# Seven products by token halves, differences in place, a bias table stored head by head, and a final norm in another order

## The chip, the cores and the metric

The kernel runs on one core of one Trainium2 chip. Its time is in device microseconds (us); runs of one kernel mostly agree within 0.3%. A core has a matrix engine (TensorE; PE in the rows, its weight loads PEld), a vector engine (VectorE, DVE), an activation engine (ScalarE, ACT), GpSimd (POOL) and SyncE (SP), which here issues every DMA. The engines run side by side, each works through its own list in order, and one that needs another's result waits at a semaphore. One DMA is shared out over up to 16 DMA engines.

## The reference, cut to what matters

One decoder layer on 1024 tokens of width 1024: a mixer sub-layer (pooling, and sparse attention with a relative bias), attention to a memory, and a SwiGLU feed-forward layer, each between two RMSNorms and added to the residual. The change touches three places:

```python
def _rmsnorm(x, g):
    y = xf * lax.rsqrt(jnp.mean(xf * xf, axis=-1, keepdims=True) + EPS)
    return (y * g).astype(x.dtype)
...
        bias = rel_bias_table[_t5_bucket(q_pos[None, :, None] - sel)]   # 8 heads, 32 buckets
        logits = logits + jnp.moveaxis(bias, -1, 1)
...
def _swiglu(h, w_gate_up, w_down):          # D_MODEL 1024, D_FF 2816
    g, u = jnp.split(h @ w_gate_up, 2, axis=-1)
    return (jax.nn.silu(g) * u) @ w_down
...
        h = _rmsnorm(x, norm_ffn_pre)
        x = x + _rmsnorm(_swiglu(h, w_gate_up, w_down), norm_ffn_post)
```

All of it is float32. The kernel splits each operand into a high and a low part and makes every product from three matmuls (high x high, high x low, low x high).

## The kernel before, in words

**Order.** Nothing is issued as it is written. A recorder (`Recorder`) notes each operation with its tiles, and a planner (`schedule`) then makes one list per engine: of the operations whose inputs are ready by its own costs it takes, for each engine, the earliest in program order that has its buffers. It prices a DMA by its bytes alone (`total * 4 / 360.0` ns). Large tiles share 42 slots of 4 KB per partition (`slot`), weights on their way have two buffers for the high part (`whi`) and two for the low (`wlo`), and 512-column products have four PSUM banks (`bank`). Since every operation is issued by one helper line, all rows carry L139; tiles are told by their names (a row leaves out trailing digits).

**The start.** Blocks of 128 tokens are normed and transposed (`pt_n`). Then come the indexer's key and queries (`o_ki`, `o_qi`); their halves are copied across partitions by DMAs (`kih`, `kil`, `qi`), after which the indexer's scores (`sc`) are made. Everything later on TensorE stands behind the first `sc` in its list. Beside this GpSimd builds one row of 383 biases for each of the 8 heads (`brow`, on 8 partitions), and a DMA writes each row 128 times to DRAM (`rowd`, 1024 rows of 1532 bytes). Attention reads it back some 300 us later (`Bn`). The weights of the pooling branch (`r_wu`) come on the same queue.

**Gate and up.** The layer's first product is done with seven half-size products instead of eight (the Winograd form of Strassen's method). The weight tile of 128 columns `f` (22 of them) gives seven weight operands; the activations are cut into B11, B21 (one half of the tokens, first and second 512 channels) and B12, B22 (the other half), and into the differences T1 = B12 - B11, T2 = B22 - T1, T3 = B22 - B12, T4 = B21 - T2. Each of the seven is split (`spread`: ScalarE high, VectorE low). In the kernel before, a token half holds every other block of 128 tokens (`divmod(b, 2)`), so blocks 0 to 3 give the first 256 columns of all seven and blocks 4 to 7 the second 256. So that TensorE has work before the last blocks are closed, the first two weight tiles (`CUT = 2`) are multiplied 256 columns at a time; the other 20 take 512 columns. One weight tile is seven products of 12 matmuls into three banks (`ga`, `gb`, `gc`). Seven weight operands of each of the first four tiles were prepared earlier and stored; `fetch` loads all seven of a tile in one go (`uw`, 512 KB each).

**Closing a block.** `close` takes the memory output `z` of a block, norms it (`j_pb`, `me_pb`, `rs_pb`), adds the residual (`zb`), stores it (`x2d`), norms it again (`j_nb`, `xn_nb`), transposes it (`pt_nb`), and ScalarE copies the transposes to `h3B..x`.

**The end.** `w_down` is multiplied in six pieces; in the last each block gets its sum (`acc`, in halves of 512), squares on ScalarE (`jf`), the gain (`acc * g6`, 1024 wide, in place, hence after both squares), the mean and power on GpSimd (`mef`, `rf`), and two multiply-adds with the residual (`x2r`) that are stored.

Of the kernel before, what the change touches and what calls it, by code (L numbers as in the profile page):

```python
# [17 lines left out]
P = 128  # L18
# [322 lines left out]
def hybrid_block_kernel(ctx: ExitStack, tc: tile.TileContext, x, mem, norm_mix_pre, norm_mix_post,  # L341
# [140 lines left out]
    class WinoT:  # L482

        TYPES = ("B11", "T2", "T1", "T3", "B21", "T4", "B22")

        def __init__(self, name):
            self.name, self.hl, self.src = name, {}, {}

        def k(self, t, c, s):
            return self.hl[t][0][c // 2][:, c % 2, s], self.hl[t][1][c // 2][:, c % 2, s]

        def close(self, src, g, b, name):
            r = rstd_of(src, name)
            xn = slot([P, D], F32, f"xn_{name}")
            apply_norm(xn, src, r, g)
            t, h = divmod(b, 2)
            v, u = divmod(t, 2)
            if h == 0 and u == 0:  # L500
                self.src[v] = {B: slot([P, 4, 2, P], F32, f"{self.name}{B}x{v}") for B in ("B11", "B21", "B12", "B22")}
            for q in range(2):
                pt = bank([P, 4, P], f"pt_{name}{q}")
                for c in range(4):
                    nc.tensor.transpose(pt[:, c], xn[:, (4 * q + c) * P:(4 * q + c + 1) * P], ident)
                nc.scalar.activation(self.src[v][f"B{q + 1}{h + 1}"][:, :, u], pt, AF.Copy)
            if h == 1 and u == 1:
                B = self.src[v]
                for T, a, b_ in (("T1", "B12", "B11"), ("T2", "B22", "T1"), ("T3", "B22", "B12"), ("T4", "B21", "T2")):
                    B[T] = slot([P, 4, 2, P], F32, f"{self.name}{T}x{v}")  # L510
                    nc.vector.tensor_tensor(B[T], B[a], B[b_], op=OP.subtract)

        def spread(self, v):
            s = slice(v * 256, (v + 1) * 256)
            for t in self.TYPES:
                if v == 0:
                    self.hl[t] = [[slot([P, 2, 512], F32R, f"{self.name}{t}{w}{j}") for j in range(2)] for w in "hl"]
                for j in range(2):
                    split(self.hl[t][0][j][:, :, s], self.hl[t][1][j][:, :, s],
                          self.src[v][t][:, 2 * j:2 * j + 2].rearrange("p c u t -> p c (u t)"))  # L520

# [102 lines left out]
    while u < span:  # L624
# [251 lines left out]

    def fetch(f):
        shapes = [[P, KC, P]] * 2 + [[P, 2, 4, P]] * 5
        ts = []
        nc.ahead = nc.SHORT  # L880
        for j, shape in enumerate(shapes):
            if j < 2:
                t = nc.tile(sb, shape, F32R, name=f"uw{f}{j}", tag=("whi", "wlo")[j], bufs=2)
            else:
                t = slot(shape, F32R, f"uw{f}{j}")
            v = f32(t) if j < 2 else f32(t).rearrange("p a c m -> p (a c) m")
            nc.sync.dma_start(v, unitd[f, j])
# [3 lines left out]

    def operands(ts):
        gh, gl, h12, l12, h34, l34, a22 = ts
        return dict(A11=(gh[:, :4], gl[:, :4]), A12=(gh[:, 4:], gl[:, 4:]), A22=(a22[:, 0], a22[:, 1]),
                    S1=(h12[:, 0], l12[:, 0]), S2=(h12[:, 1], l12[:, 1]),
                    S3=(h34[:, 0], l34[:, 0]), S4=(h34[:, 1], l34[:, 1]))
# [114 lines left out]

    units = [(i, g) for i in range(NB) for g in range(2)]
    ready = {units[0]: attn_soft(*units[0])}
    for k, (u, nxt) in enumerate(zip(units, units[1:] + [None])):
        if nxt:
            ready[nxt] = attn_soft(*nxt)
        attn_pv(*u, ready.pop(u))
        if k < 8 and k + GFIRST < KC:
            attn_gate(k + GFIRST)
        if k >= 8:  # L1020
            proj_attn(0, [k - 8])
    proj_attn(1, range(KC))
# [43 lines left out]


    KVm = [slot([P, D], F32R, f"{n}n{w}_") for n in "KV" for w in "hl"]
    for j in range(4):
# [89 lines left out]

    aTd = nc.tile(dr, [NF, P, 2, 512], F32, name="aTd", tag="aTd", dram=True)  # L1160

    def mmk(o, wh, wl, act, t, s, first):
        for c in range(4):
            ah, al = act.k(t, c, s)
# [4 lines left out]
    def gate_up(f, W, c0=0, c1=512):  # L1169
        n, s = c1 - c0, slice(c0, c1)  # L1170
        A, B, C = (bank([P, n], f"g{x}{f}{c0}") for x in "abc")
        m1, u2, u3, c22, c12, c21 = (t[:, j] for t in
                                     [nc.tile(sb, [P, 2, n], F32, name=f"g{x}{f}{c0}", tag="ld", bufs=LD) for x in "muv"]
                                     for j in range(2))

        def prod(o, a, t, first):
            mmk(o, *W[a], h3T, t, s, first)

        prod(A, "A11", "B11", True)
        nc.scalar.activation(m1, A, AF.Copy)  # L1180
        prod(B, "S2", "T2", True)
        nc.vector.tensor_tensor(u2, B, m1, op=OP.add)
        prod(C, "S1", "T1", True)
        prod(B, "S3", "T3", False)
        nc.vector.tensor_tensor(u3, B, m1, op=OP.add)
        nc.vector.tensor_tensor(c22, C, u3, op=OP.add)
        prod(A, "A12", "B21", False)
        nc.scalar.activation(u3, A, AF.Silu)
        prod(B, "A22", "T4", False)
        nc.vector.tensor_tensor(c21, B, m1, op=OP.add)  # L1190
        nc.vector.tensor_tensor(c21, c21, u3, op=OP.mult)
        nc.sync.dma_start(aTd[f, :, 0, s], c21)
        prod(C, "S4", "B22", False)
# [3 lines left out]
        nc.sync.dma_start(aTd[f, :, 1, s], c12)  # L1197
# [7 lines left out]
    get = lambda f: operands(fetch(f) if f < FIRST else gu_units(f))  # L1205
    nxt = get(CUT)
    for f in range(CUT, NF):
        cur, nxt = nxt, get(f + 1) if f + 1 < NF else None
        gate_up(f, cur)

# [4 lines left out]
    for fs in pieces:  # L1215
# [11 lines left out]
        for b in range(NB):  # L1227
            t, h = divmod(b, 2)
            qs = slice(t * P, (t + 1) * P)
# [15 lines left out]
            else:  # L1245
                xb = load(x2d[b * P:(b + 1) * P, :], f"x2r{b}")
                ms = []
# [12 lines left out]
                for n in range(2):  # L1260
                    ns = slice(n * 512, (n + 1) * 512)
                    nc.vector.scalar_tensor_tensor(acc[b][:, ns], acc[b][:, ns], r, xb[:, ns],
                                                   op0=OP.mult, op1=OP.add)
                    nc.sync.dma_start(out[b * P:(b + 1) * P, ns], acc[b][:, ns])

# [31 lines left out]
```

## Time and profile before

| | us |
|---|---|
| three runs | 1652.63, 1650.62, 1648.18 (median 1650.62) |
| the profiled execution | 1647.8 |
| its span, first to last instruction | 1646.0 |
| TensorE busy | 1582.9 (96%) |
| mean granted TensorE clock | 0.989 of full |

A busy TensorE is not one at its peak: matmuls overlap, and each row's time runs over the next one's start. A wait is printed behind a row as [us <-engine tile]; a wait for several things is put down to the one that came last. Clock rows of a window give the share of full speed that was granted.

### The profile page before, as it was taken

The page shows a single profiled execution, that of the slowest core. Times are in us where ns is not written, and L with a number is a line of the kernel's source. Part 1 is how long each engine was busy: PE and PEld are TensorE (multiplying, and loading weights), DVE is VectorE, ACT ScalarE, POOL GpSimd, SP SyncE. Part 2 cuts the span into 40 slices and gives each one's busy share as a digit, 9 for nine tenths or more (in the row PEclk, how much of TensorE's full clock was granted, in tenths as well). Part 3 has the DMA queues.
Part 4 walks back from the last instruction along what each step waited for, and adds up shares of the span by engine and source line. Part 5 has one row for each costly group of instructions (what it writes and reads, how often), then busy time and mean ns, then how long its engine had stood idle before and what let it go on. Part 6 is the DMA issues. An engine that isn't in the chain of part 4 may idle for free. (4 is left out here: it accounts for less than half of the span.)

```text
span 1646.0 us, 20711 instructions
## 1 busy us (share of the span) xinstructions
PE 1582.9 (96%) x7758; PEld 1333.1 (81%) x7758; DVE 1063.8 (65%) x1839; ACT 574.4 (35%) x970; POOL 219.7 (13%) x311
## 2 busy tenths in 40 slices
PE   4799999999999999999999979999999999999998
PEld 4687888887887888787899869888888888888886
DVE  5399888889644777457755685566555554644436
ACT  5363111212455655335436561222322222311102
POOL 7034000000123343001103220000000000000003
PEclk9899999999999999999999999999999999999999
DMA  6611322363733232289963345222222224622104
GB/s 190 105 51 40 108 76 65 103 186 127 237 117 108 72 115 77 75 279 373 384 209 130 107 176 205 89 78 95 83 78 77 90 77 160 211 103 92 62 13 154
DMA packets 184244, 213.16 MB, mean 130 GB/s; under 512 B 8656, under 2 KB 142544, under 8 KB 184144
## 3 DMA queue, kind: packets, MB, share of 16 engines
q1 hardware_dynamic: 184144, 211.84, 39.9%
q8 instruction: 61, 1.00, 0.3%
q14 instruction: 39, 0.32, 0.1%
HBM read 147.07 MB, written 63.43 MB: 128 GB/s over the span
## 5 line engine op out<-in xcount | busy, mean ns | idle before, releaser
L139 DVE TENSOR_SCALAR_CACHE_REDUCE tja<-score,canda 128x384 bf16<-128x384 f32 (+1 forms) x186 | 165.6, 941 | 0.9
L139 PE MATMUL dn<-h_wd,aTh 128*128 128x512 f32 x352 | 136.8, 389 | 0.0
L139 PE MATMUL dn<-l_wd,aTh 128*128 128x512 f32 x352 | 136.8, 389 | 0.0
L139 PE MATMUL dn<-h_wd,aTl 128*128 128x512 f32 x352 | 136.6, 389 | 0.0
L139 DVE TENSOR_TENSOR acc<-dn,acc 128x1024 f32<-128x1024 f32 (+1 forms) x48 | 50.2, 1046 | 105.5 <-PE dn L139 105.5
L139 POOL TENSOR_SCALAR mef<-ms,ms 128x1 f32<-128x1 f32 x8 | 10.6, 1321 | 651.3 <-ACT jf L139 651.3
L139 PEld LDWEIGHTS dn<-h_wd,aTl 128*128 128x128 f32 x352 | 66.1, 188 | 13.8
L139 PEld LDWEIGHTS dn<-l_wd,aTh 128*128 128x128 f32 x352 | 66.1, 188 | 13.7
L139 PEld LDWEIGHTS dn<-h_wd,aTh 128*128 128x128 f32 x352 | 66.1, 188 | 13.6
L139 DVE TENSOR_TENSOR l<-s,h 128x1024 fp32r<-128x1024 f32 x44 | 53.7, 1223 | 34.1 <-PE gc L139 31.1
L139 ACT ACTIVATE h<-s 128x1024 fp32r<-128x1024 f32 x44 | 46.5, 1062 | 82.6 <-DVE s L139 62.3
L139 POOL TENSOR_SCALAR L<-L,ri 128x128 f32<-128x128 f32 (+7 forms) x64 | 49.5, 777 | 176.2 <-DVE ri L139 134.0
L139 PE MATMUL lg<-kTh,qq 128*128 128x512 f32 (+2 forms) x192 | 58.1, 353 | 2.9 <-issue 1.5
L139 ACT ACTIVATE aTh<-at 128x1024 fp32r<-128x1024 f32 x22 | 22.8, 1051 | 104.7 <-PE dn L139 93.1
L139 PE MATMUL po<-T,Vh 128*128 128x512 f32 x144 | 54.1, 412 | 4.9 <-DVE T L139 2.6
L139 ACT ACTIVATE L<-L,nm 128x128 f32<-128x128 f32 (+7 forms) x64 | 49.7, 777 | 22.7 <-DVE nm L139 21.2
L139 DVE TENSOR_TENSOR T<-pt,T 128x512 fp32r<-128x512 f32 x72 | 46.7, 682 | 12.4 <-ACT T L139 12.0
L139 DVE CUSTOM_DVE_ANT_0 L<-lg,mb 128x256 f32<-128x256 f32 (+1 forms) x64 | 25.1, 401 | 45.8 <-PE lg L139 45.6
L139 ACT ACTIVATE h_wg<-r_wg 128x1024 fp32r<-128x1024 f32 x22 | 23.4, 1063 | 88.5 <-PE ga L139 77.9
L139 POOL TENSOR_TENSOR mb<-Bn,mask 128x1024 f32<-128x1024 f32 (+1 forms) x16 | 36.0, 2251 | 128.7 <-DMA qd<-qh 114.3
L139 PE MATMUL y<-h_wo,mgh 128*128 128x512 f32 x128 | 50.4, 394 | 0.8 <-ACT h_wo L139 0.8
L139 PE MATMUL o_ga<-hTh,h_wga 128*128 128x512 f32 x128 | 51.0, 399 | 0.0
(400 smaller groups left out, 4699.8 us busy)
## 6 DMA issues: line engine op xcount, KB each, us to landing
uw<-unitd SPq DMA_DIRECT2D x28, 512.0 KB, 8.1
r_wg<-in_w_gate_up_dram SPq DMA_DIRECT2D x22, 512.0 KB, 3.9
r_wu<-in_w_gate_up_dram SPq DMA_DIRECT2D x22, 512.0 KB, 3.9
r_wd<-in_w_down_dram SPq DMA_DIRECT2D x22, 512.0 KB, 4.5
at<-aTd SPq DMA_DIRECT2D x22, 512.0 KB, 4.8
aTd<-gv SPq DMA_DIRECT2D x40, 256.0 KB, 2.0
qq<-qd SPq DMA_DIRECT2D x32, 256.0 KB, 4.8
r_wpa<-in_w_proj_attn_dram SPq DMA_DIRECT2D x16, 512.0 KB, 4.4
```

The costliest lines, as they stand in the source:

```text
L139: op.emit = lambda: fn(*args, **kw)
```

## The change

- `WinoT.close`: the token halves are now blocks 0 to 3 and blocks 4 to 7 (`divmod(b, 4)`), so B11 and B21 are whole, 512 columns wide, when block 3 is closed. The differences are written over the sources (T1 over B11, T3 over B12, T2 over B22, T4 over B21), and each is split as soon as it is there.
- `gu_first`: for the first four weight tiles the two products that need only B11 and B21 (2 x 12 matmuls a tile) are done ahead, with their results kept in a slot (`gm`). `fetch` loads a tile's own operands (part 0) and the sums (part 1) apart. The halves of 256 columns are gone.
- The bias rows: `bias_rows(h)` stores one head's row; it is written into the program after the pooling branch's step `m`, eight DMAs of 128 rows instead of one of 1024.
- Attention: the gate products stand one unit later, and the first projection's eight steps follow the table `PROJ` (two of them in unit 14) instead of one for each unit from 8 on.
- The final norm: the gain goes into a tile of its own (`zf`), one half right behind each half of the sum.

```diff
-            t, h = divmod(b, 2)
+            h, t = divmod(b, 4)
...
+            if u == 1:
+                B11, B12, B21, B22 = (self.src.get((B, v)) for B in ("B11", "B12", "B21", "B22"))
+                if h == 0:
+                    self.spread(v, "B11", B11)
+                    self.spread(v, "B21", B21)
+                    return
+                self.spread(v, "B22", B22)
+                for T, a, b_, home in (("T1", B12, B11, B11), ("T3", B22, B12, B12), ("T2", B22, B11, B22),
+                                       ("T4", B21, B22, B21)):
+                    nc.vector.tensor_tensor(home, a, b_, op=OP.subtract)
+                    self.spread(v, T, home)
...
-    nc.sync.dma_start(rowd, bass.AP(tensor=row.tensor, offset=row.offset,
-                                    ap=[list(row.ap[0]), [0, P], [1, span]]))
+
+    def bias_rows(h):
+        nc.sync.dma_start(rowd[h:h + 1], bass.AP(tensor=row.tensor, offset=row.offset + h * row.ap[0][0],
+                                                 ap=[[row.ap[0][0], 1], [0, P], [1, span]]))
...
         nc.sync.dma_start(mAd[m], mA)
+        bias_rows(m)
...
-    def fetch(f):
+    def fetch(f, part):
...
+        for j in (range(2), range(2, 7))[part]:
...
+    PROJ = {9: (0,), 10: (1,), 11: (2,), 12: (3,), 13: (4,), 14: (5, 6), 15: (7,)}
...
+    def gu_first(f, W):
+
+        A = bank([P, 512], f"ga{f}")
+        m = slot([P, 2, 512], F32, f"gm{f}")
+        prod(A, W["A11"], "B11", True)
+        nc.scalar.activation(m[:, 0], A, AF.Copy)
+        prod(A, W["A12"], "B21", False)
+        nc.scalar.activation(m[:, 1], A, AF.Silu)
+        return m[:, 0], m[:, 1]
...
-    CUT = 2
-    W = {f: operands(fetch(f)) for f in range(CUT)}
-    for v in range(2):
-        h3T.spread(v)
-        for f in range(CUT):
-            gate_up(f, W[f], 256 * v, 256 * v + 256)
...
+    head = {f: gu_first(f, own(*fetch(f, 0))) for f in range(FIRST)}
+    nxt = get(0)
+    for f in range(NF):
         cur, nxt = nxt, get(f + 1) if f + 1 < NF else None
-        gate_up(f, cur)
+        gate_up(f, cur, head.get(f))
...
                     nc.vector.tensor_tensor(acc[b][:, ns], o[n], acc[b][:, ns], op=OP.add)
+                    nc.vector.tensor_tensor(z[:, ns], acc[b][:, ns], g6[:, ns], op=OP.mult)
...
-                nc.vector.tensor_tensor(acc[b], acc[b], g6, op=OP.mult)
```

Three places of the lists that the planner makes. First SyncE's list near the start, from the load of the memory tokens on (`rowd` is the bias table in DRAM, `r_wu` a pooling weight, `kih`, `kil` and `qi` the copies that the scores need):

```order
 L139 DMA mem_658<-in_mem_dram 128x1024
-L139 DMA rowd<-brow 1024x1x383
+L139 DMA rowd<-brow 128x1x383 x8
 L139 DMA r_wu_246<-in_w_in_dram 128x8x128
 L139 DMA kih<-kih 64x512
```

The eight stores stand where the one stood: the planner takes them as soon as `brow` is ready, not behind `mAd`, where the program has them.

Second, SyncE's list while the last four blocks are closed (`x2d` is a block's stored residual, `uw` an operand of a weight tile). Before:

```order
L139 DMA x2d<-zb_1915 128x1024
L139 DMA resb_1974<-x1d 128x1024
L139 DMA uw_2001<-unitd 128x1024
L139 DMA uw_2002<-unitd 128x1024
...
L139 DMA uw_2012<-unitd 128x1024
L139 DMA x2d<-zb_1929 128x1024
L139 DMA x2d<-zb_1947 128x1024
L139 DMA x2d<-zb_1965 128x1024
L139 DMA x2d<-zb_1979 128x1024
```

And now:

```order
L139 DMA x2d<-zb_1922 128x1024
L139 DMA resb_1997<-x1d 128x1024
L139 DMA x2d<-zb_1938 128x1024
L139 DMA x2d<-zb_1952 128x1024
L139 DMA x2d<-zb_1968 128x1024
L139 DMA uw_2027<-unitd 128x1024
L139 DMA uw_2028<-unitd 128x1024
L139 DMA x2d<-zb_2002 128x1024
L139 DMA uw_2031<-unitd 128x1024
L139 DMA uw_2032<-unitd 128x1024
L139 DMA uw_2035<-unitd 128x1024
```

Before, ten loads of 512 KB stand ahead of the last four stores; now two do (the third tile's own operands, 2027 and 2028), and only ahead of the last store, and the sums (2035 on) come after all of them.

Third, VectorE's list at its end, the last block (`dn` is the bank of a half, `acc` the sum, `g` the gain). Before:

```order
L139 TENSOR_TENSOR acc_2425<-dn_2641,acc_2425 128x512
L139 SCALAR_TENSOR_TENSOR acc_2423<-acc_2423,rf_2640,x2r_2634 128x512 x2
L139 TENSOR_TENSOR acc_2425<-dn_2642,acc_2425 128x512
L139 TENSOR_TENSOR acc_2425<-acc_2425,g_2397 128x1024
L139 SCALAR_TENSOR_TENSOR acc_2425<-acc_2425,rf_2649,x2r_2643 128x512 x2
```

And now:

```order
L139 TENSOR_TENSOR acc_2409<-dn_2632,acc_2409 128x512
L139 SCALAR_TENSOR_TENSOR zf_2625<-zf_2625,rf_2631,x2r_2624 128x512 x2
L139 TENSOR_TENSOR zf_2635<-acc_2409,g_2381 128x512
L139 TENSOR_TENSOR acc_2409<-dn_2633,acc_2409 128x512
L139 TENSOR_TENSOR zf_2635<-acc_2409,g_2381 128x512
L139 SCALAR_TENSOR_TENSOR zf_2635<-zf_2635,rf_2641,x2r_2634 128x512 x2
```

The gain of the first half now stands ahead of the second half's sum, and only 512 columns of it are left behind that sum.

## Rows read from the trace of the kernel before

**Rows 1.** The page: the span, and busy time of the matrix engine.
```profile
span 1646.0 us, 20711 instructions
PE 1582.9 (96%) x7758; PEld 1333.1 (81%) x7758; DVE 1063.8 (65%) x1839; ACT 574.4 (35%) x970; POOL 219.7 (13%) x311
```

**Rows 2.** Windows: stretch, length; engines' busy time (instructions); clock, DMA share, GB/s.
```profile
50.00:75.00 25.00, 18.02 (x87) 14.90 (x85) 4.63 (x9) 4.31 (x10) 0.78 (x2) 0.91 0.66 113
75.00:100.00 25.00, 23.59 (x129) 20.80 (x130) 20.17 (x31) 17.64 (x25) 3.33 (x5) 0.88 0.28 72
...
950.00:975.00 25.00, 20.01 (x111) 17.10 (x109) 17.09 (x18) 12.62 (x27) 10.05 (x14) 0.93 0.58 232
975.00:1000.00 25.00, 20.95 (x158) 19.23 (x159) 22.44 (x38) 14.03 (x27) 0.00 (x0) 1.00 0.05 16
```

**Rows 3.** TensorE's waits: tile, what ended them, total us, times, longest.
```profile
PE pt_n L139 <- DVE xn_n L139: 12.4, 5, 8.5
PE sc L139 <- DMA kih<-kih: 8.4, 1, 8.4
...
PE pt_nb L139 <- DVE xn_nb L139: 4.1, 2, 3.7
PE po L139 <- DVE T L139: 2.6, 4, 1.4
```

**Rows 4.** Timeline of TensorE before the scores: start, us, what.
```profile
67.20 0.82 PE L139 MATMUL pw<-ident,ki 128*128 128x128 f32 x6
76.42 0.66 PE L139 MATMUL sc<-kih,qi 128*128 128x384 f32 x1 [8.40 <-DMA kih<-kih]
```

**Rows 5.** Timeline of SyncE's queue, same stretch: start, us that issuing took.
```profile
35.60 0.81 SPq L139 DMA_DIRECT2D rowd<-brow  x1
37.92 8.20 SPq L139 DMA_DIRECT2D r_wu<-in_w_in_dram  x1
46.18 15.34 SPq L139 DMA_DIRECT2D kih<-kih  x1
```

**Rows 6.** DMA from 30 to 80 us: GB/s in 40 slices, the issue, KB.
```profile
GB/s 98 315 13 0 0 23 51 50 50 51 51 65 50 69 192 101 51 50 51 51 51 57 50 65 53 78 76 50 50 81 286 250 242 249 207 203 175 134 215 62
...
rowd<-brow SPq DMA_DIRECT2D x1, 1532.0 KB
```

**Rows 7.** Windows: the bias store alone, and a store of mA alone (columns as in 2).
```profile
50.00:58.00 8.00, 8.00 (x41) 6.77 (x40) 1.22 (x3) 1.94 (x6) 0.78 (x2) 1.00 0.45 52
163.90:164.90 1.00, 1.00 (x7) 0.81 (x5) 1.00 (x3) 0.00 (x0) 0.00 (x0) 1.00 0.47 188
```

**Rows 8.** The chain that ended last: products of 256 and of 512 columns.
```profile
996.15 1.44 PE gb L139 x12
...
1020.49 2.72 PE gb L139 x12
```

**Rows 9.** Timeline of TensorE: last memory product, then block 7's last transposes.
```profile
962.47 0.39 PE L139 MATMUL z<-h_wom,oTl 128*128 128x512 f32 x1
...
978.18 0.66 PE L139 MATMUL pt_nb<-ident,xn_nb 128*128 128x128 f32 x4 [0.17 <-ACT h3B12x L139]
```

**Rows 10.** Timeline of ScalarE in the same place.
```profile
961.46 0.60 ACT L139 ACTIVATE h3B11x<-pt_nb 128x512 f32<-128x512 f32 x1 [9.22 <-DMA x2d<-zb]
```

**Rows 11.** Timeline of SyncE's queue in the same place.
```profile
942.79 7.49 SPq L139 DMA_DIRECT2D uw<-unitd  x10
951.22 21.52 SPq L139 DMA_DIRECT2D x2d<-zb  x4
```

**Rows 12.** Timeline of GpSimd: the mean of a block, undisturbed and at the end.
```profile
963.63 0.22 POOL L139 TENSOR_SCALAR me_pb<-ms_pb 128x1 f32<-128x1 f32 x1 [7.93 <-ACT j_pb L139]
...
1639.59 1.32 POOL L139 TENSOR_SCALAR mef<-ms,ms 128x1 f32<-128x1 f32 x1 [3.47 <-ACT jf L139]
```

**Rows 13.** Timeline of VectorE: the gain of the last block.
```profile
1639.53 1.22 DVE L139 TENSOR_TENSOR acc<-acc,g 128x1024 f32<-128x1024 f32 x1 [0.87 <-ACT jf L139]
```

More of the change, by code (lines that the diff above doesn't have):

```diff
@@ L497, in close @@
             apply_norm(xn, src, r, g)
-            t, h = divmod(b, 2)
+            h, t = divmod(b, 4)
             v, u = divmod(t, 2)
-            if h == 0 and u == 0:
-                self.src[v] = {B: slot([P, 4, 2, P], F32, f"{self.name}{B}x{v}") for B in ("B11", "B21", "B12", "B22")}
             for q in range(2):
+                B = f"B{q + 1}{h + 1}"
+                if u == 0:
+                    self.src[B, v] = slot([P, 4, 2, P], F32, f"{self.name}{B}x{v}")
                 pt = bank([P, 4, P], f"pt_{name}{q}")
@@ L505, in close, with spread @@
                     nc.tensor.transpose(pt[:, c], xn[:, (4 * q + c) * P:(4 * q + c + 1) * P], ident)
[L506 to L513, printed above, removed]
-            s = slice(v * 256, (v + 1) * 256)
[L515 to L520, printed above, removed]
+                nc.scalar.activation(self.src[B, v][:, :, u], pt, AF.Copy)
+            if u == 1:
[9 more added lines that the diff above has]
+                    self.spread(v, T, home)
+        def spread(self, v, t, src):
+            s = slice(v * 256, (v + 1) * 256)
+            if t not in self.hl:
+                self.hl[t] = [[slot([P, 2, 512], F32R, f"{self.name}{t}{w}{j}") for j in range(2)] for w in "hl"]
+            for j in range(2):
+                split(self.hl[t][0][j][:, :, s], self.hl[t][1][j][:, :, s],
+                      src[:, 2 * j:2 * j + 2].rearrange("p c u t -> p c (u t)"))
     class QuartT:
@@ L875, in store @@
             nc.sync.dma_start(unitd[f, j], v)
-    def fetch(f):
-        shapes = [[P, KC, P]] * 2 + [[P, 2, 4, P]] * 5
+    def fetch(f, part):
         ts = []
         nc.ahead = nc.SHORT
-        for j, shape in enumerate(shapes):
-            if j < 2:
-                t = nc.tile(sb, shape, F32R, name=f"uw{f}{j}", tag=("whi", "wlo")[j], bufs=2)
-            else:
-                t = slot(shape, F32R, f"uw{f}{j}")
-            v = f32(t) if j < 2 else f32(t).rearrange("p a c m -> p (a c) m")
+        for j in (range(2), range(2, 7))[part]:
+            if part == 0:
+                t = nc.tile(sb, [P, KC, P], F32R, name=f"uw{f}{j}", tag=("whi", "wlo")[j], bufs=2)
+                v = f32(t)
+            else:
+                t = slot([P, 2, 4, P], F32R, f"uw{f}{j}")
+                v = f32(t).rearrange("p a c m -> p (a c) m")
             nc.sync.dma_start(v, unitd[f, j])
@@ L890, in fetch, with own, sums @@
         return ts
[L892 to L895, printed above, removed]
+    def own(gh, gl):
+        return dict(A11=(gh[:, :4], gl[:, :4]), A12=(gh[:, 4:], gl[:, 4:]))
+    def sums(h12, l12, h34, l34, a22):
+        return dict(A22=(a22[:, 0], a22[:, 1]), S1=(h12[:, 0], l12[:, 0]), S2=(h12[:, 1], l12[:, 1]),
                     S3=(h34[:, 0], l34[:, 0]), S4=(h34[:, 1], l34[:, 1]))
@@ L1017, in hybrid_block_kernel @@
         attn_pv(*u, ready.pop(u))
[L1018 to L1021, printed above, removed]
+        if 0 < k <= KC - GFIRST:
+            attn_gate(k + GFIRST - 1)
+        for m in PROJ.get(k, ()):
+            proj_attn(0, [m])
     proj_attn(1, range(KC))
@@ L1065, in hybrid_block_kernel @@
     pend()
+    aTd = nc.tile(dr, [NF, P, 2, 512], F32, name="aTd", tag="aTd", dram=True)
     KVm = [slot([P, D], F32R, f"{n}n{w}_") for n in "KV" for w in "hl"]
@@ L1157, in hybrid_block_kernel, with prod @@
     pend()
-    aTd = nc.tile(dr, [NF, P, 2, 512], F32, name="aTd", tag="aTd", dram=True)
-    def mmk(o, wh, wl, act, t, s, first):
+    def prod(o, w, t, first):
+        wh, wl = w
         for c in range(4):
-            ah, al = act.k(t, c, s)
+            ah, al = h3T.k(t, c)
             nc.tensor.matmul(o, wh[:, c], ah, start=first and c == 0, stop=False, skip_group_check=True)
@@ L1167, in mmk @@
             nc.tensor.matmul(o, wl[:, c], ah, start=False, stop=c == 3, skip_group_check=True)
[L1169 to L1181, printed above, removed]
+    def gu_first(f, W):
[6 more added lines that the diff above has]
+        return m[:, 0], m[:, 1]
@@ new lines, in gate_up @@
+    def gate_up(f, W, head=None):
+        A, B, C = (bank([P, 512], f"g{x}{f}") if head is None or x != "a" else None for x in "abc")
+        (m1, u2), (u3, c22), (c12, c21) = ([t[:, j] for j in range(2)] for t in [
+            nc.tile(sb, [P, 2, 512], F32, name=f"g{x}{f}", tag="ld", bufs=LD) for x in "muv"])
+        if head is None:
+            prod(A, W["A11"], "B11", True)
+            nc.scalar.activation(m1, A, AF.Copy)
+        else:
+            m1, c11 = head
+        prod(B, W["S2"], "T2", True)
@@ L1182, in gate_up @@
         nc.vector.tensor_tensor(u2, B, m1, op=OP.add)
-        prod(C, "S1", "T1", True)
-        prod(B, "S3", "T3", False)
+        prod(C, W["S1"], "T1", True)
+        prod(B, W["S3"], "T3", False)
         nc.vector.tensor_tensor(u3, B, m1, op=OP.add)
         nc.vector.tensor_tensor(c22, C, u3, op=OP.add)
-        prod(A, "A12", "B21", False)
-        nc.scalar.activation(u3, A, AF.Silu)
-        prod(B, "A22", "T4", False)
+        if head is None:
+            prod(A, W["A12"], "B21", False)
+            c11 = u3
+            nc.scalar.activation(c11, A, AF.Silu)
@@ L1190, in gate_up @@
+        prod(B, W["A22"], "T4", False)
         nc.vector.tensor_tensor(c21, B, m1, op=OP.add)
-        nc.vector.tensor_tensor(c21, c21, u3, op=OP.mult)
-        nc.sync.dma_start(aTd[f, :, 0, s], c21)
-        prod(C, "S4", "B22", False)
+        nc.vector.tensor_tensor(c21, c21, c11, op=OP.mult)
+        nc.sync.dma_start(aTd[f, :, 0], c21)
+        prod(C, W["S4"], "B22", False)
         nc.vector.tensor_tensor(c12, C, u2, op=OP.add)
@@ L1196, in gate_up, with get @@
         nc.vector.tensor_tensor(c12, c12, c22, op=OP.mult)
-        nc.sync.dma_start(aTd[f, :, 1, s], c12)
-    CUT = 2
-    W = {f: operands(fetch(f)) for f in range(CUT)}
-    for v in range(2):
-        h3T.spread(v)
-        for f in range(CUT):
-            gate_up(f, W[f], 256 * v, 256 * v + 256)
-    get = lambda f: operands(fetch(f) if f < FIRST else gu_units(f))
-    nxt = get(CUT)
-    for f in range(CUT, NF):
+        nc.sync.dma_start(aTd[f, :, 1], c12)
+    def get(f):
+        if f < FIRST:
+            return sums(*fetch(f, 1))
+        ts = gu_units(f)
+        return dict(**own(*ts[:2]), **sums(*ts[2:]))
+    head = {f: gu_first(f, own(*fetch(f, 0))) for f in range(FIRST)}
+    nxt = get(0)
+    for f in range(NF):
         cur, nxt = nxt, get(f + 1) if f + 1 < NF else None
-        gate_up(f, cur)
+        gate_up(f, cur, head.get(f))
     g6 = gain(norm_ffn_post, "g6")
@@ L1227, in hybrid_block_kernel @@
         for b in range(NB):
-            t, h = divmod(b, 2)
+            h, t = divmod(b, 4)
             qs = slice(t * P, (t + 1) * P)
@@ L1246, in hybrid_block_kernel @@
                 xb = load(x2d[b * P:(b + 1) * P, :], f"x2r{b}")
-                ms = []
+                ms, z = [], slot([P, D], F32, f"zf{b}")
                 for n in range(2):
@@ L1261, in hybrid_block_kernel @@
                     ns = slice(n * 512, (n + 1) * 512)
-                    nc.vector.scalar_tensor_tensor(acc[b][:, ns], acc[b][:, ns], r, xb[:, ns],
-                                                   op0=OP.mult, op1=OP.add)
-                    nc.sync.dma_start(out[b * P:(b + 1) * P, ns], acc[b][:, ns])
+                    nc.vector.scalar_tensor_tensor(z[:, ns], z[:, ns], r, xb[:, ns], op0=OP.mult, op1=OP.add)
+                    nc.sync.dma_start(out[b * P:(b + 1) * P, ns], z[:, ns])
     with tc.manual_schedule():
```

5 lines of the change are left out of this document (2 added, 3 removed).

## The prediction

> **What bounds the kernel now.** I read the page first: TensorE is busy for 1582.9 of 1646.0 us [rows 1]. So only the places where it waits can give time, and only what makes it wait can cost any. Windows of 25 us show where these are: the first 100 us, and 950 to 1000 us, where TensorE works 20.01 and 20.95 of 25 us; the granted clock is below full in the same windows [rows 2]. The list of its waits, longest first, names the causes [rows 3]: 12.4 us of the first blocks' transposes `pt_n`, ahead of all that is changed; one wait of 8.4 us of the first scores (`sc`) for a DMA; and 4.1 us of the transposes `pt_nb` in the closing of the last blocks. The rest is small. After 1018 us the chain of waits holds nothing but matmuls until the final norm.
>
> The 8.4 us come from the bias table. TensorE is done with `pw` at 68.02 us and starts `sc` at 76.42 [rows 4]. The copies that `sc` needs were issued late, because SyncE's queue was stuck: issuing one weight took 8.20 us and issuing the first copy of `kih` 15.34 us, both right behind the store of `rowd` at 35.60 us [rows 5]. The view of the DMAs shows that store as a plateau of 50 to 51 GB/s from about 37 to 67.5 us, and a burst of over 200 GB/s behind it [rows 6]. 1024 rows of 1532 bytes are 1.569 MB; at 51 GB/s that is 30.8 us, the plateau's length. `sc` starts 76.42 - 67.5 = 8.9 us behind its end: the weights and copies that were queued behind it.
>
> **The bias rows, the term that decides.** The program has the eight stores 20 us apart behind the pooling steps, but SyncE's list has them at one place, where the one store was, ahead of `r_wu`, `kih`, `kil` and `qi`. So nothing is moved out of the way; the question is what eight stores of 128 rows cost, back to back. Before, while the store ran alone, the 16 engines were busy for 0.45 of the time, about 7.2 of them, and moved 52 GB/s: 7.2 GB/s each. A store of `mA` from all 128 partitions moves 188 GB/s at a share of 0.47, which is 25.0 GB/s for each busy engine [rows 7]. So the seven or eight engines of the bias store together do the work of two (52 / 25.0 = 2.1); they wait for something that they share, and what sets this store apart is that all its bytes come from eight neighbouring partitions. I take it that reading these has room for two engines' pace, 25.5 GB/s for each four partitions. One head's row lies in one partition; then a strip runs at 25.5 GB/s however many engines draw on it, and the eight, one after the other, take 1.569 MB / 25.5 = 61.5 us instead of 30.8. Everything behind them in the rings comes 30.7 us later, `sc` at 107 us. TensorE's list has the scores next, ScalarE's and VectorE's lists need them, and after 100 us TensorE has no slack to give back: +30.7 us.
>
> The bounds, by the nearest rows: if each engine keeps its 7.2 GB/s and all 16 take part, the strips take 1.569 / 115 = 13.6 us, are done by 51 us, and the wait of 8.4 us goes: -8.4. If 51 GB/s is what this destination takes, nothing changes: 0. If a single partition has only an eighth of 51 GB/s, the strips take 245 us: +214. I take +30.7, because two engines' pace for eight partitions is what rows 7 show, and one partition cannot have more than its share of them.
>
> [...]
>
> **Gate and up.** 12 matmuls of 512 columns take 2.72 us, 12 of 256 columns 1.44 [rows 8]. Two weight tiles had 14 products in two halves: 28 x 1.44 = 40.3 us; now 14 x 2.72 = 38.1. TensorE is the bound there: -2.2.
>
> **The closing of the last blocks.** From the last `z` matmul (962.47 us) to block 7's last transposes (978.18) pass 15.7 us [rows 9], the chain of norm, residual and second norm. TensorE had 45 matmuls of 256 columns to fill them, 45 x 0.12 = 5.4 us, and 24 transposes for some 2 us. One reason why the chain is that long: ScalarE waited 9.22 us for a store `x2d` [rows 10], which stood in SyncE's queue behind ten loads of 512 KB [rows 11]. In the new lists these loads come behind the stores, and between the same two points stand 58 matmuls of 512 columns, 13.1 us. TensorE's loss in that stretch shrinks from 15.7 - 5.4 - 2 = 8.3 to at most 15.7 - 13.1 - 2 = 0.6 us: 7.7 us to be had. What is new against it: the third tile's own operands wait for the first tile's buffers and are on the path after some 12 us; the first tile's second product waits for ScalarE's copy of the first, which now stands behind six splits; and T2 needs T1 in place, one subtraction of 1.1 us later. I take 1 us off for these: -6.5. Bounds: 0 if these waits eat the gain, -11 if the waits after 978 us (TensorE is busy for only 20.95 of 25 us there [rows 2]) go too. The sums are loaded after the stores; 13.6 us of products a tile stand beside 2.6 MB, and DMAs have moved over 200 GB/s [rows 6], 13 us: hidden, but with little to spare; if not, some us for each of the four tiles.
>
> **The end.** The last mean on GpSimd takes 1.32 us where such a one takes 0.22 [rows 12]; it ran beside VectorE's gain of 1.22 us over two SBUF operands, begun 0.06 us earlier [rows 13]. The gain's second half is now 512 wide and stands right behind the sum, over when the squares are; the mean should take 0.22: -1.1. Between 0 and -1.2.
>
> **Attention.** The changed table moves the fillers by a unit; TensorE's waits there are single cases of up to 1.5 us (the `po` row of [rows 3] is the largest group, 2.6 us in all). No row favours either order: 0, between -3 and +3. The other edits (differences in place, the token halves, the readback) issue as many instructions as before on engines that are not the bound.
>
> **The sum.** The profiled execution took 1647.8 us (span 1646.0). 1647.8 + 30.7 - 2.2 - 6.5 - 1.1 = 1668.7. The median of the runs shown is 2.8 above the profiled execution (1650.62): 1671.5.
>
> **The rivals.**
> - *The strips cost what the one store cost.* The limit is then the writing to DRAM, in rows of 1532 bytes. For it: total bytes and destination are the same. Against: stores of `mA` run at 188 GB/s. The wait stays 8.4 us and the rest remains: 1671.5 - 30.7 = 1640.8, faster.
> - *The strips spread over all engines.* Each engine is slow on rows of 1532 bytes, and twice as many work. For it: 0.45 of 16 engines were busy, eight idle. Against: 7.2 GB/s an engine, against 25.0 elsewhere, for rows that are not short. The wait goes: 1640.8 - 8.4 = 1632.4, faster.
> - *The strips do still worse*, one partition having less than 25.5 GB/s. At half of it, 123 us: 1671.5 + 61.5 = 1733. For it: eight partitions gave 51 in all, and how they share it no row tells.
> - *The closing loses instead of gaining*, because the sums arrive late: +5 to +10 on any of these; with the main case 1680 to 1685.
> - *The change does not do what it says*: that the bias rows are not moved is in the lists already and is part of the forecast.
>
> **How the numbers follow.** Main case 0.64, with its own range of 1660 to 1686 (strips +25 to +34, closing 0 to -11). Unchanged strips 0.14 (1634 to 1647), spread strips 0.12 (1626 to 1640), worse strips 0.05, a slip in the closing 0.05. A measurement of this kernel can tell some 0.3%, 5 us, from no change. Faster: 0.14 + 0.12 less the 0.02 where the closing gives nothing, 0.24. Same: 0.03. Slower: 0.73. The range for 8 in 10 takes the main case, the slip and most of the unchanged strips: 1634 to 1686.
>
> **What would show it.** In the changed trace: a plateau of about 25 GB/s from 37 to about 98 us, `kih` issued or landing near its end, and the wait of `sc` near 39 us instead of 8.4. At 51 GB/s until 67 the first rival holds; above 100 GB/s and no wait of `sc`, the second. In the closing: no wait of ScalarE for `x2d`, `pt_nb` of the last block within 15 us of the last `z`, products of 2.72 us throughout. At the end: `mef` at 0.22 us. I am wrong if `sc` starts by 80 us.

## The result: slower, as forecast, with a smaller loss and a larger gain

| | us |
|---|---|
| before, 4 runs | 1651.05 (1648.18 to 1652.63) |
| after, 4 runs | 1662.98 (1662.58 to 1663.96) |
| ratio | 1.0075, 95% interval 1.0058 to 1.0093 |
| forecast | 1671.5 (1634 to 1686), slower with 0.73 |

The time is 0.75% longer, clear of no change. The likeliest case came in: the eight stores run at the pace of one partition (28 GB/s) and hold up the first scores. It cost 5.9 us less than forecast, and the closing gave 3.7 us more.

The page of the profile after begins with the span, then busy time of each engine:

```profile
span 1661.1 us, 20370 instructions
PE 1576.4 (95%) x7590; PEld 1321.0 (80%) x7590; DVE 1063.7 (64%) x1833; ACT 575.3 (35%) x966; POOL 206.5 (12%) x311
```

The span is 15.1 us longer than that of [rows 1], while TensorE has 6.5 us less to do. So it is idle for 21.6 us more. The list of its waits after (tile, what ended them, total us, times, longest) says where:

```profile
PE sc L139 <- DMA qi<-qil: 33.2, 1, 33.2
...
PE po L139 <- DVE T L139: 5.1, 7, 1.8
...
PE pt_nb L139 <- DVE xn_nb L139: 0.6, 1, 0.6
```

Against [rows 3], the scores' wait has grown from 8.4 to 33.2 us, that of the attention product `po` from 2.6 to 5.1, and that of the closing's transposes has shrunk from 4.1 to 0.6.

**The start.** TensorE's timeline after, first scores (start, us, what, [wait before it]), and SyncE's queue in the same stretch (start, us that issuing took):

```profile
101.22 0.66 PE L139 MATMUL sc<-kih,qi 128*128 128x384 f32 x1 [33.23 <-DMA qi<-qil]
```

```profile
35.20 41.10 SPq L139 DMA_DIRECT2D rowd<-brow  x8
76.40 7.11 SPq L139 DMA_DIRECT2D r_wu<-in_w_in_dram  x1
83.62 7.27 SPq L139 DMA_DIRECT2D kih<-kih  x1
```

SyncE is held for 41.10 us by issuing the eight stores alone; the one store took it 0.81 us [rows 5]. `kih`, issued over 46.18 to 61.52 us before, is issued at 83.62. In the view of the DMAs from 30 to 130 us (GB/s in 40 slices of 2.5 us) and in a window inside the plateau (columns as in [rows 2]) the pace can be read:

```profile
GB/s 213 0 17 27 26 28 27 27 26 28 31 34 28 34 44 34 23 29 29 29 21 28 42 44 138 289 250 196 159 111 45 165 0 0 96 120 0 0 0 0
...
rowd<-brow SPq DMA_DIRECT2D x8, 191.5 KB, 24.7
```

```profile
38.00:60.00 22.00, 18.32 (x97) 16.77 (x98) 10.02 (x18) 7.56 (x17) 3.35 (x5) 0.79 0.87 28
```

The engines' share is 0.87 now, 14 of 16 where about 7 were busy before, and together they move 28 GB/s instead of 52 [rows 7]: twice the engines, half the bytes. The plateau ends near 90 us, and the scores start some 10 us behind it, as they did before.

**Where the rest lies.** The first memory output `z` and the T2 products of the fifth weight tile (row of a tile: us of one, first and last start). Before:

```profile
L139 PE MATMUL z<-h_wom,oTh x64: 389/389/500, 895.9 to 962.0; 128*128 128x512 f32 x64
L139 PE MATMUL gb<-h3T2h,h x72: 389/389/389, 1058.4 to 1384.1; 128*128 128x512 f32 x72
```

After:

```profile
L139 PE MATMUL z<-h_wom,oTh x64: 389/389/504, 924.4 to 988.8; 128*128 128x512 f32 x64
L139 PE MATMUL gb<-h3T2h,h x72: 389/389/389, 1074.5 to 1400.2; 128*128 128x512 f32 x72
```

| point | before | after | later by |
|---|---|---|---|
| first scores | 76.42 | 101.22 | 24.8 |
| first `z` | 895.9 | 924.4 | 28.5 |
| first T2 product, fifth tile | 1058.4 | 1074.5 | 16.1 |
| last product of `w_down` | 1637.54 | 1653.63 | 16.1 |
| end of the span | 1646.0 | 1661.1 | 15.1 |

So, by these two traces, the bias stores cost 24.8 us, attention 3.7, the closing and the gate products give 12.4, and the end gives 1.0. Windows over the third stretch (columns as in [rows 2]) tell what the 12.4 us are. Before:

```profile
895.90:962.47 66.57, 65.72 (x378) 56.71 (x378) 42.41 (x50) 35.52 (x76) 18.43 (x30) 1.00 0.44 160
962.47:1058.40 95.93, 87.73 (x538) 78.32 (x537) 64.80 (x98) 37.61 (x67) 4.88 (x10) 0.98 0.36 130
```

After:

```profile
924.40:989.10 64.70, 64.69 (x374) 56.15 (x373) 42.31 (x53) 37.78 (x80) 15.25 (x34) 1.00 0.24 86
989.10:1074.50 85.40, 83.28 (x375) 67.68 (x374) 59.62 (x80) 32.51 (x53) 4.98 (x6) 1.00 0.59 205
```

TensorE's idle time there falls from 162.5 - 153.45 = 9.05 us to 150.1 - 147.97 = 2.1 us, and its busy time by 5.5 us. ScalarE's wait for `x2d` (9.22 us in [rows 10]) is gone. A part of the busy time is the clock. In one stretch before, right behind TensorE's wait of 3.69 us for a block's norm, the granted clock was 0.50 of full:

```profile
968.40:971.60 3.20, 3.20 (x16) 2.98 (x15) 3.17 (x5) 2.89 (x7) 0.93 (x3) 0.50 0.40 164
```

Twelve products of 256 columns took 2.86 us there (968.44 to 971.30), where [rows 8] have 1.44. After, the clock is 1.00 throughout. At the end, the last mean on GpSimd and the last half of the gain on VectorE after:

```profile
1655.69 0.29 POOL L139 TENSOR_SCALAR mef<-ms,ms 128x1 f32<-128x1 f32 x1 [4.50 <-ACT jf L139]
```

```profile
1654.79 0.69 DVE L139 TENSOR_TENSOR zf<-acc,g 128x512 f32<-128x512 f32 x1
```

The gain is over before the mean starts, and the mean takes 0.29 us instead of 1.32 [rows 12].

### The profile page after: what moved, and what is told of

It reads as the page before. It is cut to its first block, busy times and chain, and to the rows that moved or that the text cites. A ratio compares the mean times of both kernels' runs of the same rounds, so it can differ in the third digit from the quotient of the medians.

```text
span 1661.1 us, 20370 instructions
## 1 busy us (share of the span) xinstructions
PE 1576.4 (95%) x7590; PEld 1321.0 (80%) x7590; DVE 1063.7 (64%) x1833; ACT 575.3 (35%) x966; POOL 206.5 (12%) x311
## 4 chain that ended last, share of the span: by engine, by line
PE 83%; DVE 5%; SPq 4%; DMA 3%; issue 2%; ACT 2%; POOL 2%; DVEq 0%; POOLq 0%; ACTq 0%
PE dn L139 14%; PE gb L139 11%; PE gc L139 7%; PE ga L139 7%; PE o_q L139 5%; PE o_ga L139 5%; PE o_gp L139 5%; PE y L139 4%; SPq L139 4%; PE o_pa L139 4%; PE po L139 3%; PE z L139 3%; PE qm L139 3%; PE ap L139 3%; PE lg L139 2%
## 5 line engine op out<-in xcount | busy, mean ns | idle before, releaser
L139 POOL TENSOR_SCALAR mef<-ms,ms 128x1 f32<-128x1 f32 x8 | 2.4, 296 | 643.2 <-ACT jf L139 643.2
L139 ACT ACTIVATE T<-pt 128x512 fp32r<-128x512 f32 x72 | 39.2, 597 | 36.4 <-PE pt L139 34.4
```

Of the source, the lines that this page charges most:

```text
L139: op.emit = lambda: fn(*args, **kw)
```

## The experiments

Each stands against the kernel before on the same chip (1648.6 to 1649.0 us, 9 to 15 runs; the result above had 1651.05), so that its ratio is the safer number.

**1. The bias stores, undone and alone.** In `e1_one_store` the changed kernel has its old store back; in `e2_strips_alone` the kernel before has only the eight stores. The edit of the first (the second's is its reverse):

```diff
-    def bias_rows(h):
-        nc.sync.dma_start(rowd[h:h + 1], ...)      # 128 rows, called after each mAd[m]
+    nc.sync.dma_start(rowd, bass.AP(..., ap=[list(row.ap[0]), [0, P], [1, span]]))
```

> The changed kernel with the one store of 1024 bias rows back in place of the eight; the lists of all engines are otherwise the same. My theory (the eight stores run one after the other at 28 GB/s and hold up everything behind them in SyncE's queue; nothing later gives the time back): the plateau is 50 to 52 GB/s again and ends near 67.5 us, the first scores wait 8 us instead of 33.2, and the time is 1663.0 - 24.8 = 1638 us. Rival (the stores only shift a wait, and the 24.8 us would be lost elsewhere without them): 1650 us or more.

> The kernel before with the eight stores as its only edit. My theory: the first scores start at 101 us, and the time is 1651.0 + 24.8 = 1676 us. Rival (in the changed kernel the stores meet other traffic that the edit brought): less than half of that, below 1663.

Measured: 1638.64 us, 0.9943 of before (0.9929 to 0.9956), and 1673.86, 1.0155 (1.0139 to 1.0171). The scores' wait in the two:

```profile
PE sc L139 <- DMA qi<-qil: 9.6, 1, 9.6
```

```profile
PE sc L139 <- DMA qi<-qil: 33.5, 1, 33.5
```

Both rivals are out. Beside the rest of the edit the stores cost 24.3 us by the times (1662.98 - 1638.64) and some 22 us by the ratios (1.0075 - 0.9943 of 1650); alone they cost 25.3 us (1673.86 - 1648.58). Without them the change is a gain.

**2. The same bytes from other partitions.** The lists of TensorE, VectorE, ScalarE and SyncE are those of `e1_one_store` (GpSimd's has one memset more); only the eight heads' partitions differ, by a step of 16, 2 and 4 (the table is built on 128, 16 and 32 partitions):

```diff
-    tabT = nc.tile(sb, [HEADS, NBUCK], ...)
+    step, rows = 16, 128
+    tabT = nc.tile(sb, [rows, NBUCK], ...); nc.gpsimd.memset(tabT, 0.0)
...
-        ap=[list(row.ap[0]), [0, P], [1, span]]
+        ap=[[step * row.ap[0][0], HEADS], [0, P], [1, span]]
```

> As the run with one store, but the eight rows of the table lie on partitions 0, 16, 32 to 112 instead of 0 to 7 (the table is built on 128 partitions); one store, the same bytes to the same place, in the same rows of 1532 bytes. My theory (the partitions that a store reads set its pace, neighbours share): the store runs at over 150 GB/s and is over before 48 us, the wait of the first scores goes from 8.4 to under 1, and the time is 1638 - 8.4 = 1630 us. Rival (the limit is the destination, or rows of 1532 bytes): 50 to 52 GB/s as before, 1638 us.

> As the run before it, but the rows lie on partitions 0, 2, 4 to 14. My theory, that partitions share in fours: twice as many fours, so twice 51 GB/s: a plateau of about 104 GB/s that ends near 52 us, the first scores start at 68 to 70 us, 1630 us. Rivals: if the limit is the number of partitions, or eight neighbours share, it stays at 51 GB/s and 1638 us; if it is the destination, the same.

> As the run with one store, but the eight rows of the table on partitions 0, 4, 8 to 28. Partitions 0, 2 to 14 gave 107 GB/s and 0, 16 to 112 gave 96, where eight neighbours gave 51 and one partition 28. My theory (partitions share in fixed groups of four neighbours, and groups that lie 32 or 64 apart share too or not, which step 16 left open): here are eight groups within 32 partitions, so 170 to 210 GB/s, the store over before 46 us. Rival (7 to 8 engines with rows of 1532 bytes do not do more than about 107 GB/s, whatever the partitions): 96 to 108 GB/s as with steps 2 and 16. In both cases no wait of the first scores above 3 us and 1623 to 1628 us, since 107 GB/s was enough to hide the store.

Windows inside the store (second to last column: share of the DMA engines' time; last: GB/s), for partitions 0 to 7 (`e1_one_store`), then for step 16, step 2 and step 4:

```profile
38.00:42.00 4.00, 0.22 (x1) 0.25 (x2) 4.00 (x5) 0.00 (x0) 1.89 (x1) 0.50 0.45 51
```

```profile
38.00:42.00 4.00, 3.18 (x26) 2.98 (x25) 3.68 (x6) 3.21 (x9) 3.89 (x3) 1.00 0.47 96
```

```profile
37.80:41.20 3.40, 0.00 (x0) 0.00 (x0) 3.40 (x3) 0.00 (x0) 2.05 (x1) 0.53 0.48 106
```

```profile
37.80:41.20 3.40, 2.66 (x12) 2.66 (x13) 3.20 (x5) 2.48 (x5) 3.31 (x3) 0.54 0.55 186
```

| partitions read | GB/s | time, us | ratio, interval |
|---|---|---|---|
| one at a time (after) | 28 | 1662.98 | 1.0075, 1.0058 to 1.0093 |
| 0 to 7 (`e1`) | 51 | 1638.64 | 0.9943, 0.9929 to 0.9956 |
| 0, 16 to 112 (`e3`) | 96 | 1623.58 | 0.9849, 0.9836 to 0.9863 |
| 0, 2 to 14 (`e4`) | 106 | 1627.38 | 0.9872, 0.9858 to 0.9885 |
| 0, 4 to 28 (`e5`) | 186 | 1621.79 | 0.9830, 0.9816 to 0.9843 |

In the last four rows one store brings the same 1024 rows of 1532 bytes to the same place; only where they are read differs, and the pace goes from 51 to 186 GB/s. That the destination or the row length holds it at 51 is excluded. Steps 2 and 4 came out as fours of neighbours would have it: 106 where 104 was expected, 186 where 170 to 210 was. Step 16 did not: I expected over 150 GB/s from eight groups, and 96 are no more than step 2 gave with four. So these eight would share in pairs; which with which, no run here tells. One partition gave 28 GB/s, two groups 51 and four 106, some 25.5 to 28 a group (an estimate: these paces divided by the groups); eight would make 212 (an estimate, twice the 106), and 186 were measured. At step 4 the share of 0.55 is about 9 engines with 21 GB/s each, not far from the 25.0 of [rows 7], so there it may be the engines that limit; that was not tested.

All three hide the store; the wait of the scores is gone with steps 2 and 4 and is 2.5 us with step 16. All three times lie 1 to 6 us below what was expected. And steps 4 and 16 are faster than step 2, though step 16 stores more slowly than step 2. So the store is not the whole of it, which led to the next run.

**3. A norm on VectorE that takes 7.17 us beside GpSimd.** In the runs with 8 or 16 partitions a norm (`xn_n`) on VectorE takes 7.17 us, in those with 32 and 128 it takes 1.27. `e11_step2_rows32` is step 2 with one number changed: `step, rows = 2, 32` instead of `2, 16`.

> The run with the heads on partitions 0, 2 to 14 (1627.4 us), but the table is built by instructions on 32 partitions instead of 16; the stored rows and their partitions are the same. With 8 and 16 partitions a norm on VectorE at 34 us took 7.17 us, with 32 and 128 it took 1.27, beside the same list of GpSimd. Theory (the width of GpSimd's instructions decides which of the two engines gets through, and this is the whole difference between steps 2 and 4): the norm takes 1.27 us, the plateau is 107 GB/s as before, and the time is 1627.4 - 5.6 = 1622 us. Rival (it hangs on when the store or something else starts): 7.17 us and 1627 us.

Measured: 1623.26 us, 0.9849 (0.9836 to 0.9862), against 0.9872 for step 2. VectorE's and GpSimd's timelines with 16 partitions, then the same with 32:

```profile
33.76 7.17 DVE L139 SCALAR_TENSOR_TENSOR xn_n<-x,rs_n,g 128x1024 f32<-128x1024 f32 x1
```

```profile
33.18 2.05 POOL L139 TENSOR_SCALAR brow<-brow,tabD 16x1 f32<-16x1 f32 x8
35.21 4.64 POOL L139 TENSOR_TENSOR l_wki<-r_wki,h_wki 128x1024 fp32r<-128x1024 f32 x2
```

```profile
33.85 1.27 DVE L139 SCALAR_TENSOR_TENSOR xn_n<-x,rs_n,g 128x1024 f32<-128x1024 f32 x1
```

```profile
33.27 3.01 POOL L139 TENSOR_SCALAR brow<-brow,tabD 32x1 f32<-32x1 f32 x8
36.25 4.75 POOL L139 TENSOR_TENSOR l_wki<-r_wki,h_wki 128x1024 fp32r<-128x1024 f32 x2
```

TensorE feels it in the transposes `pt_n`, which wait longer for the low halves `hTl`. Its wait for them with 16 partitions, then with 32:

```profile
PE pt_n L139 <- DVE hTl L139: 9.1, 2, 7.1
```

```profile
PE pt_n L139 <- DVE hTl L139: 2.4, 2, 2.0
```

With 16 partitions VectorE's instruction ends at 40.9, about a microsecond behind the end of all ten of GpSimd's (39.85); with 32 it ends at 35.12, while GpSimd is still at its eight, and these take 3.01 us instead of 2.05. The theory held in kind. In size it gave 4.1 us of the 5.6 expected, and the first scores start 4.1 us earlier (62.66 instead of 66.75); the last 1.5 us between steps 2 and 4 are within what the two intervals leave open. The stall and TensorE's wait stand in the kernel before too:

```profile
34.11 7.17 DVE L139 SCALAR_TENSOR_TENSOR xn_n<-x,rs_n,g 128x1024 f32<-128x1024 f32 x1
```

```profile
PE pt_n L139 <- DVE hTl L139: 8.3, 2, 6.3
```

There the scores wait for the store anyway, so taking the stall away alone should gain little; no run tried it.

**4. The stores where the program has them.** In `e12_strips_late` each store waits for one of 4 bytes that reads `mA`:

```diff
         nc.sync.dma_start(mAd[m], mA)
+        nc.sync.dma_start(rowd[m, 0:1, 0:1], mA[0:1, 0:1])
         bias_rows(m)
```

> The changed kernel with the eight stores, of one partition each, really made at the place where the program has them: each waits for a store of 4 bytes that reads the pooling branch's tile, so SyncE's list has them from 180 us on, among the weights of the later products. Theory (28 GB/s for 7 us each, beside loads that are hundreds of us ahead of their use, delay nothing): no wait of the first scores above 2 us, and 1627 us, as with the heads on partitions 0, 2 to 14. Rival (SyncE waits for the small stores, and the weights behind them come late): TensorE waits for weights between 150 and 450 us, and 1632 us or more.

Measured: 1627.46 us, 0.9872 (0.9858 to 0.9885). Six of the stores, issued from 181.97 to 260.59 us, stand 13 to 16 us apart; in the window below the pace is 26 GB/s, like the 28 of the change; no scores wait for a DMA. One issue of a store, and a window inside one:

```profile
195.24 0.49 SPq L139 DMA_DIRECT2D rowd<-brow  x1
```

```profile
182.50:186.00 3.50, 3.50 (x17) 2.88 (x17) 2.61 (x7) 1.41 (x2) 0.00 (x0) 1.00 0.75 26
```

So it takes both to lose the time. Early in the list the eight slow stores cost some 24 us more than the one store there (experiment 1); where the program has them, as slow as they are, they are harmless.

**5. Feed-forward, attention and norm, each alone on the kernel before.** `e8_ffn_alone` has the change's `close`, `spread`, `fetch` and `gu_first`, `e6_table_alone` its `PROJ` table and the gate's place, `e10_norm_alone` its final norm, as the change's diff shows them.

> The kernel before with the feed-forward edit as its only one (token halves, differences in place, two products of four weight tiles ahead, no halves of 256 columns). Theory (closing and gate products together gave 12.4 us: the shift of 28.5 us at the first memory output has become 16.1 at the fifth weight tile): 12.4 us less than the kernel before, 0.9925 of its time. Rival (the gain needs the late start or the new attention order): under half of that. If the 2.2 us forecast for the wider products is right, TensorE's busy time from the first memory output to the fifth tile is less by more than that, and its waits there fall from 8 to about 2 us.

> The kernel before with the changed attention table as its only edit (gate products one unit later, two projection steps in unit 14). Theory (the table itself loses time: from the first scores to the first memory output pass 819.5 us in the kernel before, 817.9 with the eight stores alone, but 823.2 and 823.5 in the two kernels that have the table): +3.7 us against the kernel before, 1.002 of its time. Rival (the loss comes from the shifted start or from the feed-forward part, whose loads come earlier in SyncE's list): no difference, within 0.1%.

> The kernel before with the final norm's edit as its only one, one look. Theory: the last mean on GpSimd takes 0.3 us instead of 1.3, and from the last product of w_down to the end of the span pass 1.0 us less, 1 us on the whole, too little to be told from the times. Rival: the gain's two halves keep VectorE from the next sum, and the end comes no earlier.

Measured: feed-forward 1636.49 us, 0.9922 (0.9909 to 0.9934), 12.5 us less, as in the changed kernel; from the first `z` to the fifth tile TensorE is busy for 5.5 us less and idle for 2.3 us instead of 9.05. How this gain is shared among the edit's parts (the order of the stores, the products ahead, the wider products) was not separated. Table 1652.09, 1.0020 (1.0011 to 1.0029), 3.1 us more. Two of its waits:

```profile
PE po L139 <- DVE T L139: 4.9, 6, 1.8
PE km L139 <- DVE l_wkm L139: 3.5, 1, 3.5
```

The wait of `po` for `T` goes with the table: 2.6 us in every run without it, 4.8 to 5.1 with it; but the runs without it have another 1.5 us of `po` waiting for `nm`. That of `km` is 0.3 to 1.8 us without and 2.0 to 3.5 with it, and moves by 1.5 us between runs whose lists are the same up to there. Over all traces the stretch from the first scores to the first `z` takes 817.9 to 822.0 us without the table (five runs) and 820.4 to 823.5 with it (nine), so some of the 3.7 us read from two traces is scatter. The 3.1 us are the safer number.

Norm, in one run: 1647.5 us; from the last product of `w_down` to the end of the span pass 7.4 us instead of 8.5, 1.1 us less, and the mean takes 0.29 us. The times alone can't tell that. The three parts add up to -10.5 us; the changed kernel with its old store has 9.9 us less than the kernel before (experiment 1).

`e7_best` is the kernel with step 4 and the table of before:

> The run with the heads on partitions 0, 4 to 28, with the attention table of the kernel before instead of the changed one. Theory (the table costs 3.1 to 3.8 us wherever the start lies): 1621.8 - 3.4 = 1618.4 us, 0.981 of the kernel before. Rival (it costs them only behind the old start): 1622, 0.983.

Measured: 1620.92 us, 0.9828 (0.9815 to 0.9842), against 0.9830 with the changed table. The number is the rival's, but the interval reaches to 0.9815 and so does not exclude the theory's 1618.4 us (0.9817). The traces side with the rival: from the first scores to the first `z` pass 819.6 us, against 820.4 with the changed table. So behind the early start the table's price can't be told from nothing. What it costs there stays open.

**6. Are the products ahead hidden?** `e9_short_fillers` is step 4 with 36 of the 96 matmuls of `gu_first` not issued, those of the third and fourth tile (a part of the gate's and up's products is then missing from the result); everything else stands as it did:

```diff
+        if f > 1:
+            for op in [those matmuls but the first two and the last of each product]:
+                op.emit = lambda: None
```

> The run with the heads on partitions 0, 4 to 28; of the 24 products ahead of the third and fourth weight tile 18 are left out for each (36 matmuls of 512 columns, 8.2 us of TensorE; so part of the feed-forward result is not computed). All lists are otherwise the same. Theory (these products stand beside the closing of the last block, whose chain of norm, transposes, differences and splits ends at the same time as they do): TensorE waits for T2 instead, and the time falls by less than 2.5 us. Rival (TensorE's list sets the pace there, the products could stand anywhere): it falls by all 8.2 us, to 1613.6.

Measured: 1623.07 us, 0.9841 (0.9828 to 0.9855), against 0.9830 with all of them: leaving 8.2 us of TensorE's work out saves nothing. From the first `z` to the fifth tile with all of them, and without the 36:

```profile
882.80:1033.70 150.90, 148.14 (x747) 123.84 (x747) 101.95 (x131) 70.15 (x133) 20.20 (x40) 1.00 0.43 152
```

```profile
883.70:1034.20 150.50, 142.69 (x711) 118.11 (x710) 101.92 (x131) 70.05 (x133) 20.25 (x40) 0.99 0.43 153
```

The stretch is 0.4 us shorter, and TensorE's idle time in it grows from 2.8 to 7.8 us. It waits instead, in the closing, for norm, T1 and T2 above all:

```profile
PE pt_nb L139 <- DVE xn_nb L139: 2.5, 2, 1.9
PE gc L139 <- DVE h3T1l L139: 1.4, 1, 1.4
PE ga L139 <- ACT gm L139: 1.2, 2, 0.7
PE gb L139 <- ACT h3T2h L139: 1.0, 1, 1.0
```

So these 36 matmuls are free: they fill time in which TensorE would wait for the chain of the last block, which is what ends last. The other 60 were not tried.

## Why the prediction was right, and where its sizes were off

- **The bias stores (+30.7 forecast, +24.8 in the trace, 22 to 25 by experiment 1).** The mechanism was the one forecast, place and all: a plateau of one partition's pace, `kih` issued near its end, the scores behind it. Mis-sized was the pace, 25.5 GB/s taken as half of the old store's 51; one partition alone gave 28, so the eight take 56 us and not 61.5. The scores started at 101.2 instead of 107. No run shows the 25.5 GB/s for each four partitions, or that one partition has them alone; both were my guess from the rows, and in their place the runs showed 28 for one partition and 51 for eight neighbours. The rival of a half pace (1733) is out by the 28 GB/s, that of a destination's limit by experiment 2. The rival of spread engines was half right: 14 engines were busy (0.87 of 16), and it helped nothing. The program has the stores some 16 us apart, not 20; nothing hung on it.
- **Gate, up and the closing (-2.2 - 6.5 = -8.7 forecast, -12.4 measured).** Idle time fell by 6.9 us, close to the 6.5. The busy time fell by 5.5 where 2.2 were taken for the wider products. The granted clock explains some 1.5 us of the rest (an estimate: twelve matmuls took 2.86 us instead of 1.44 while it was 0.50, and four more ran then). The prediction saw that the clock was below full there, but priced the 45 matmuls of the closing at full pace (0.12 us each) and gave the clock no term. The remaining 1.8 us were not separated. The sign "within 15 us of the last `z`" was wrong: block 7's last transposes start 18.2 us behind it (989.22 to 1007.42), because TensorE's list has the products ahead in front of them and TensorE is idle for only some 2 us meanwhile. Experiment 6 shows for 36 of these matmuls that they cost nothing. The rival in which the closing loses has a slip in its sum: 5 to 10 us on 1671.5 are 1676.5 to 1681.5, not 1680 to 1685.
- **The end (-1.1 forecast, -1.0 measured)**, as described.
- **Attention (0 plus or minus 3 forecast, +3.7 in the trace, 3.1 by `e6_table_alone`)**, at or just outside its own bounds. The table is the cause behind the start of before (1.0020 alone); behind an early start no cost can be told (`e7_best`).
- **A wait passed over.** Among TensorE's waits the prediction calls all the rest small behind the three it names. It left out 8.3 us of `pt_n` for `hTl`. The change did not touch it, so the forecast did not suffer, but once the store is out of the way it holds up the scores, and experiment 3 got 4.1 us there.
- The terms together miss by -5.9 - 3.7 + 3.7 + 0.1 = -5.8 us of the 8.5 between 1671.5 and 1662.98; that the closing and attention miss by the same amount in opposite directions is luck. The rest is the 2.8 us that I added because the median of before lies above its profiled execution; the changed kernel's profiled execution, 1662.9 us, lies at its median.

## What to carry to other kernels

Here a table in eight neighbouring partitions was stored at 51 GB/s, the same table 4 partitions apart at 186 and one partition at a time at 28: with such a table, try where its rows lie before thinking of splitting the store. A planner that issues whatever is ready while its queue is idle, and prices a DMA by its bytes alone, puts such a store ahead of what is urgent; where an operation is written later in the program, read in the list whether it is later there. And try each part of a change alone: here one part hid 12 us of gain under 25 us of loss, and the best of the runs is 1620.92 us, 0.9828 of before (0.9815 to 0.9842), with 1621.79 us (0.9830) no different.

## What was not expected of the hardware

- Eight partitions 16 apart gave 96 GB/s, not more than eight 2 apart (106), while eight 4 apart gave 186.
- SyncE was held for 41.10 us by issuing eight DMAs of 192 KB in a row, and for 7.11 us by the weight behind them. Where they stood 13 to 16 us apart (`e12_strips_late`), six of the same eight took 0.49 to 0.50 us each, and a store of `mA` issued at 186.40 us, while one of them was under way, took 0.35. So one such store under way did not hold the issuing and eight in a row did; what holds it is not shown.
- A VectorE norm of 1.27 us took 7.17 beside GpSimd instructions on 8 or 16 partitions, and 1.27 beside the same ones on 32 or 128. Why the width decides is not shown.
